# Ranking instructions by due time, a two-round selection for the first block, and three pieces of elementwise work moved to ScalarE, in a two-layer hybrid encoder

## The chip, the cores and the metric

The kernel runs on one core of one Trainium2 chip. The core has a matrix engine (TensorE, PE in the profile, with its weight loads as PEld), VectorE (DVE), ScalarE (ACT), GpSimd (POOL) and SyncE (SP, which issues the DMAs). Each engine works through its own list in the order in which the program gives it. The metric is the time of one execution on the device in microseconds (us).

## The reference, cut to what matters

The input is 512 frames of width 1024, with 16 learned meta tokens ahead of them. There are two layers, and after them a last normalization. In float32:

```python
# layer 1: sparse attention (8 heads) beside gated linear attention (4 heads)
score = einsum(relu(iq . ik), iw) * IDX_SCALE       # the indexer, per query over all keys
score = where(admissible, score, -1e30)
idx   = top_k(score, 128)                           # 128 keys for each query
logits = q . k[idx] / 8 + rel_bias                  # per head
p = softmax(where(ok, logits, -1e30)); oa = p @ v[idx]
ob = head_rms(gla_chunked(bq, bk, bv, log_a))
h = h + (concat(oa * silu(ag), ob * silu(bg)) @ w_out_ab)
# layer 2: retention (4 heads) beside stick-breaking attention (8 heads)
z = q . k / 8                                       # keys before the query only
log_1m = -softplus(z)                               # max(z,0) + ln(1 + exp(-|z|)), negated
w = exp(log_sigmoid(z) + (reverse_cumsum(log_1m) - log_1m)); od = w @ v
oc = head_layer_norm(retention(cq, ck, cv))
h = h + (concat(oc * silu(cg), od * silu(dg)) @ w_out_cd)
y = rms_norm(h)
```

Queries come in four blocks of 128. Block b sees 16 + 128(b+1) keys: 144, 272, 400 and 528.

## The kernel before

Every product in float32 accuracy is made of three: a weight tile `raw` (128x512) is split into a high part `wh` (a rounded copy made by ScalarE in `hi`) and a low part `wl` (`raw - wh`, made by VectorE in `lo`), the activations are split into `hh` and `hl` once per layer, and TensorE adds up hh.wh, hl.wh and hh.wl in a PSUM tile `acc` (two buffers). One projection of 128 columns is 8 such steps ("ticks"). Smaller products go to the PSUM tiles `x` (three buffers, shared by scores and transposes) and `y` (one).

Layer 1 plays its parts in the order of the string `V G0 G1 D A0 A1 C0 C1 A2 A3 C2 C3` after the indexer: values, two pairs of gated linear attention heads, the end of the selection (D), then four pairs of attention heads (A) and their gates (C). Layer 2 plays `V S0 S1 R0 S2 S3 R1`: S is a pair of stick-breaking heads, R a pair of retention heads. `out_ab` and `out_cd` are the out-projections.

**Selection** (`topk`). Each of the four blocks has a tile `score` (kind `lt`). A round finds the eight greatest of each row (`max`, which the trace shows as MAX8) and overwrites them with a mark (`match_replace`: MATCH_VALUE_LOAD and MATCH_REPLACE8). Sixteen rounds mark 128 keys; a last `tensor_scalar` turns marked into 0 and the others into -1e30, which the attention adds to its logits. The rounds of the four blocks take turns.

**Attention and stick-breaking** work on units: blocks 0 and 1 together (416 columns), block 2 (400), block 3 (528, in two PSUM tiles of 272 and 256). For softmax, ScalarE makes the exponentials with their sums, VectorE the reciprocal, and VectorE multiplies by it. For a stick-breaking unit, ScalarE makes |z| from PSUM, VectorE copies z out of PSUM and then makes max(z, 0) from the copy (tile `m`), ScalarE makes ln(1 + exp(-|z|)), VectorE adds up backwards over the keys (a scan that reads `m`), subtracts, and ScalarE exponentiates. Then TensorE transposes the weights and multiplies by the values.

**The order of the work.** No instruction is issued when the code calls it. A `Recorder` notes all of them in the order of the code (`o.at`), with their dependences; in that order chains of small steps are mixed into the projections by the tick. Two readers of one PSUM tile on different engines are noted as a dependence too. Then `order` plays a model of the five engines, with a cost for each instruction from `price`, and picks for each engine again and again the listed instruction with the least

```python
key = (max(est + (self.MARGIN if e == "tensor" else 0) - base, 0.0), o.pri)
```

where `est` is when the instruction could start by the model and `base` when the engine is free. Among instructions that could start at once, `o.pri` decides, and it is the place in the code. (The two subtractions from it in `add` are by `EVICT` and `SPLIT`, both 0.) Buffers of one kind are handed out in the order of the code. `issue` then emits everything in the order found; all of it has line 373 in the trace, so the trace is read by tile names.

Of the kernel before, what the change touches and what calls it, by code (L numbers as in the profile page):

```python
# [9 lines left out]
F32 = mybir.dt.float32  # L10
F32R = mybir.dt.float32r
I32 = mybir.dt.int32
AF = mybir.ActivationFunctionType
ALU = mybir.AluOpType
AX = mybir.AxisListType

P = 128
DM = 1024
KT = DM // P
NMETA = 16  # L20
# [5 lines left out]
NEG = -1e30  # L26
# [99 lines left out]
class RecordedPool:  # L126
# [4 lines left out]
    def tile(self, shape, dt, tag=None, bufs=1, name=None):  # L131
        fixed = tag is None
        tag = tag or name
        n = 1
        for y in shape[1:]:
            n *= y
        if tag not in self.kinds:
            k = self.kinds[tag] = Kind()
            width = max(n, {"tiny": 32, "mid": P}.get(tag, 0))
            k.width, k.pool, k.tag = width, self.pool, tag  # L140
            k.free = [(0.0, i) for i in range(bufs)]
            k.any = self.pool.tile(shape, dt, name=tag) if fixed else k.buffer(0, F32)
        k = self.kinds[tag]
        t = Held(k, shape, dt, self.psum, self.whole)
        t.width = k.width
        if fixed:
            t.fixed, t.buf = True, k.any
        return View(t, (), t.shaped(k.any))
# [17 lines left out]
class Recorder:  # L166
# [6 lines left out]
    def add(self, eng, name, args, kw):  # L173
        o = Op()
        o.eng, o.name, o.args, o.kw = eng, name, args, kw
        views = [x for x in args if isinstance(x, View)]
        outs = [x for x in args[:1] if isinstance(x, View)]
        if name == "tensor_tensor_reduce":
            outs.append(args[7])
        if isinstance(kw.get("accum_out"), View):  # L180
            outs.append(kw["accum_out"])
        ins = [x for x in list(args[1:]) + list(kw.values()) if isinstance(x, View) and not any(x is y for y in outs)]
        if name == "copy_predicated":
            ins.append(args[0])
        o.outs, o.ins = outs, ins
        o.at = o.pri = len(self.ops)
        kinds = {x.tile.kind.tag for x in outs + ins}
        if eng != "tensor":
            o.pri -= self.EVICT if "acc" in kinds else self.SPLIT if kinds & {"wh", "wl"} else 0
        o.preds, o.succs, o.tiles = {}, [], []  # L190
        for write, xs in ((False, ins), (True, outs)):
            for x in xs:
                self.depend(o, x, write)
        self.price(o)
        self.ops.append(o)
# [22 lines left out]
    def price(self, o):  # L218
        o.mm, o.port = None, False
        n = max([x.free() for x in o.ins + o.outs] or [1])  # L220
        sbuf = not any(x.tile.psum for x in o.ins)
        scalar = 65 if any(isinstance(x, View) and x.free() == 1 for x in o.ins) and n > 1 else 0
        if o.eng == "tensor":
            lhs, rhs = (o.args[1], o.args[2]) if len(o.args) > 2 else (o.kw["lhsT"], o.kw["rhs"])
            turn = o.name == "transpose"
            plain = rhs.dtype == F32
            k, m, n = lhs.shape[0], lhs.free(), rhs.free()
            two = plain and not turn
            o.mm = (k, plain, max(n * 0.452 * (2 if two else 1) + 2, 107 * m / P + 2) + (107 if two and n <= P else 0))
            o.cost = max(273, 170 + 0.4375 * n) if not two else 180 + 1.62 * n  # L230
        elif o.eng == "scalar":
            o.cost = (205 if sbuf else 165) + 0.83 * n + (80 if isinstance(o.kw.get("bias"), View) or isinstance(o.kw.get("scale"), View) else 0)
            if "accum_out" in o.kw:
                o.cost += 200
        elif o.eng == "vector":
            o.port = sbuf and o.name not in ("max", "match_replace")
            if o.name == "tensor_tensor_scan":
                o.cost = 144 + 2.1 * n
            elif o.name in ("tensor_scalar", "tensor_copy") and sbuf:
                o.cost = 160 + 0.52 * n + scalar  # L240
            elif o.name == "memset":
                o.cost = 100 + 0.3 * n
            else:
                o.cost = 148 + 1.05 * n + scalar
            if o.name == "tensor_tensor_reduce" or "accum_out" in o.kw:
                o.cost += 80
            if o.name == "match_replace":
                o.cost += 70
        elif o.eng == "gpsimd":
            o.cost = {"memset": 92 + 0.84 * n, "tensor_tensor": 178 + 2.17 * n}.get(o.name, 194 + 1.5 * n)  # L250
        else:
            x = o.outs[0] if o.outs else o.ins[0]
            kb = n * x.shape[0] / 256
            o.cost = 2000 + kb * (9 if any(y.tile.whole for y in o.outs + o.ins) else 3.5)
# [3 lines left out]
    OVER = {"vector": -84, "scalar": -103, "gpsimd": -60}  # L258
    SWITCH, ROWS = 86, 50
    MARGIN = 300  # L260
    EVICT = 0
    SPLIT = 0
    SLACK = {"tensor": 0, "vector": 0, "scalar": 0, "gpsimd": 0, "sync": 0}

    def order(self):
        ops = self.ops
        for o in ops:
            o.wait = len(o.preds)
            for q in o.preds:
                q.succs.append(o)  # L270
        ends = {}
        free = dict.fromkeys(self.LAT, 0.0)
        lists = {e: [] for e in self.LAT}
        last = None
        pool_until = 0.0
        begun = {}
        result = []

# [98 lines left out]
class Kernel:  # L377
# [488 lines left out]
    def topk(self):  # L866

        nc = self.nc
        for b in range(NB):
            nk = NMETA + P * (b + 1)  # L870
            nc.gpsimd.memset(self.score[b][0:64, nk - 64:nk], NEG)
        for r in range(TOPK // 8):
            for b in range(NB):
                nk = NMETA + P * (b + 1)
                sc = self.score[b][:, :nk]
                m8 = self.sm.tile([P, 8], F32, tag="m8", bufs=4, name=self.name("m8"))
                nc.vector.max(m8, sc)
                nc.vector.match_replace(sc, m8, sc, MARK)
                yield self.TOPY
        for b in range(NB):  # L880
            nk = NMETA + P * (b + 1)
            sc = self.score[b]
            nc.vector.tensor_scalar(sc[:, :nk], sc[:, :nk], -2e38, NEG, op0=ALU.is_gt, op1=ALU.mult)
            nc.gpsimd.memset(sc[0:64, nk - 64:nk], NEG)
            yield 1

# [223 lines left out]
    def attention_steps(self, p, qs, ks, kl, strips, gates):  # L1110
# [6 lines left out]
        def scores(odd, u, ws):  # L1117
# [28 lines left out]
            for i, (b, c0) in enumerate(blocks):  # L1146
                nk = NMETA + P * (b + 1)
                nc.vector.tensor_scalar(pm[:, b, odd], bm[:, c0:c0 + NMETA], sums[:, i:i + 1], None, op0=ALU.mult)
                c = slice(c0 + NMETA, c0 + nk)
                nc.vector.tensor_scalar(bm[:, c], bm[:, c], sums[:, i:i + 1], None, op0=ALU.mult)  # L1150
                ws[odd, b] = bm[:, c0:c0 + nk]
            if u == 0:
                s = self.s()
# [416 lines left out]
    def stick_steps(self, p, qs, ks, kl, gates):  # L1570
# [3 lines left out]
        def scores(odd, u, ws):  # L1574
            blocks, banks = self.UNITS[u]
            l, m, z = self.wt(), self.wt(), self.wt()
            w = sum(k1 - k0 for prods in banks for _, k0, k1 in prods)
            for s, at, prods in self.qk_banks(banks, qs[odd], ks[odd], kl[odd], frames=True):
                n = s.shape[1]
                c = slice(at, at + n)  # L1580
                s0 = 0
                for b, k0, k1 in prods:
                    s0 += k1 - k0
                    if k1 == NMETA + P * (b + 1):
                        nc.vector.tensor_tensor(s[:, s0 - P:s0], s[:, s0 - P:s0], self.strict, op=ALU.add)
                nc.scalar.activation(l[:, c], s, AF.Abs)
                nc.vector.tensor_copy(z[:, c], s)
                if at + n < w:
                    yield 1
            nc.vector.tensor_scalar(m[:, :w], z[:, :w], 0.0, None, op0=ALU.max)  # L1590
            nc.scalar.activation(l[:, :w], l[:, :w], AF.Exp, scale=-1.0)
            nc.scalar.activation(l[:, :w], l[:, :w], AF.Ln, bias=self.one[:, 0:1])
            for b, c0 in blocks:
                c = slice(c0, c0 + NMETA + P * (b + 1))
                mv, lv = m[:, c], l[:, c]
                nc.vector.tensor_tensor_scan(mv[:, ::-1], mv[:, ::-1], lv[:, ::-1], 0.0, ALU.add, ALU.add)
                ws[odd, b] = mv
            nc.vector.tensor_tensor(m[:, :w], z[:, :w], m[:, :w], op=ALU.subtract)
            nc.scalar.activation(m[:, :w], m[:, :w], AF.Exp)
            for b, c0 in blocks:  # L1600
                nc.vector.tensor_copy(pm[:, b, odd], m[:, c0:c0 + NMETA])
            yield 1
# [160 lines left out]
```

## Time and profile before

| | |
|---|---|
| time, median of 3 runs | 668.94 us (668.85 to 668.98) |
| profiled execution, its own time | 667.77 us |
| its span, first to last instruction | 666.0 us |
| PE busy | 635.4 us (95%), 4469 matmuls |
| PEld busy | 580.6 us (87%) |
| DVE busy | 507.4 us (76%) |
| ACT busy | 383.1 us (58%) |
| POOL busy | 74.9 us (11%) |
| mean granted TensorE clock | 0.988 |
| chain that ended last | PE 68%, DVE 17%, ACT 9%, issue 3% |

Busy time is the union of an engine's instructions. Matmuls are pipelined and overlap, so that a wait shorter than a matmul doesn't show as idle time of PE. A granted clock of 1.00 is TensorE's upper level (2.4 GHz), 0.50 its lower one (1.2 GHz); a stretch with a value between holds some of each.

### The profile page before, as it was taken

To read this page: it belongs to the slowest core of one execution; us is meant where nothing else is said; L and a number is where in the kernel's file an instruction comes from. 1 tells how busy PE (TensorE), PEld (TensorE's weight loads), DVE (VectorE), ACT (ScalarE), POOL (GpSimd) and SP (SyncE) were. 2 spreads that over 40 slices of the span, in tenths; PEclk is the share of its full clock that TensorE was granted. 3 is DMA by queue.
4 is the path that set the end of the run, shared out by engine and by line. 5 is a ranking of instruction groups with operands and counts; after the bars stand their busy time and mean duration, and the time that the engine had idled before them with its cause. 6 is when DMAs were issued, how large, how long until landed. Compare 5 with 4: busy or idle time off the path is not lost.

```text
span 666.0 us, 12243 instructions
## 1 busy us (share of the span) xinstructions
PE 635.4 (95%) x4469; PEld 580.6 (87%) x4469; DVE 507.4 (76%) x1273; ACT 383.1 (58%) x846; POOL 74.9 (11%) x124
## 2 busy tenths in 40 slices
PE   6999999899999999999999999998999999899996
PEld 5979999799889999999899898877888879887884
DVE  5767799999998879799532854999846799865543
ACT  4656663353335667586443765888554797644434
POOL 7000100120110010001211200000200000110030
PEclk8999999999999999999999999999999999799999
DMA  8437223223214222231242453121222213224403
GB/s 238 110 82 226 64 64 96 49 81 90 57 34 121 75 67 74 64 96 48 71 124 72 159 157 90 49 76 48 74 75 64 64 32 90 70 64 153 148 17 126
DMA packets 91103, 59.25 MB, mean 89 GB/s; under 512 B 7314, under 2 KB 81628, under 8 KB 91044
## 3 DMA queue, kind: packets, MB, share of 16 engines
q1 hardware_dynamic: 91044, 58.48, 30.5%
q8 instruction: 35, 0.57, 0.3%
q14 instruction: 24, 0.20, 0.1%
HBM read 53.18 MB, written 6.90 MB: 90 GB/s over the span
## 4 chain that ended last, share of the span: by engine, by line
PE 68%; DVE 17%; ACT 9%; issue 3%; DMA 1%; SPq 1%; POOL 0%; POOLq 0%; ACTq 0%; DVEq 0%
PE acc L373 46%; PE x L373 15%; PE y L373 6%; ACT wt L373 4%; DVE wt L373 3%; DVE lt L373 3%; DVE m L373 3%; DVE st L373 3%; DVE wl L373 2%; ACT st L373 2%; ACT wh L373 1%; SPq L373 1%; DVE pt L373 1%; DMA pt<-in_x_dram 1%; ACT pt L373 1%
## 5 line engine op out<-in xcount | busy, mean ns | idle before, releaser
L373 PE MATMUL acc<-hh,wh 128*128 128x272 f32 (+2 forms) x968 | 242.9, 312 | 1.7 <-DVE st L373 0.5
L373 PE MATMUL acc<-hl,wh 128*128 128x272 f32 (+2 forms) x968 | 234.9, 303 | 0.1
L373 PE MATMUL acc<-hh,wl 128*128 128x272 f32 (+2 forms) x968 | 233.0, 302 | 0.0
L373 ACT ACTIVATE wh<-raw 128x512 fp32r<-128x512 f32 x152 | 95.3, 629 | 124.6 <-PE acc L373 106.7
L373 PEld LDWEIGHTS acc<-hh,wh 128*128 128x128 f32 x968 | 158.2, 190 | 9.7 <-issue 1.4
L373 PEld LDWEIGHTS acc<-hh,wl 128*128 128x128 f32 x968 | 157.7, 189 | 5.6 <-issue 0.4
L373 PEld LDWEIGHTS acc<-hl,wh 128*128 128x128 f32 x968 | 157.7, 189 | 4.8 <-DVE hl L373 0.6
L373 DVE TENSOR_TENSOR wl<-raw,wh 128x512 fp32r<-128x512 f32 x153 | 111.0, 732 | 50.9 <-ACT wh L373 49.7
L373 POOL TENSOR_TENSOR gt<-gt,wt 128x528 f32<-128x528 f32 (+1 forms) x16 | 21.8, 1361 | 321.4 <-ACT wt L373 251.2
L373 PE MATMUL x<-ident,wt 128*128 128x128 f32 (+2 forms) x300 | 48.1, 278 | 7.7 <-DVE wt L373 4.5
L373 PE MATMUL x<-st,st 128*128 128x272 f32 (+6 forms) x240 | 50.9, 290 | 0.6 <-DVE pt L373 0.4
L373 ACT ACTIVATE wt<-x 128x272 f32<-128x272 f32 (+3 forms) x68 | 29.3, 434 | 34.3 <-PE x L373 22.4
L373 ACT ACTIVATE wt<-wt 128x528 f32<-128x528 f32 (+3 forms) x74 | 43.0, 593 | 9.2 <-DVE wt L373 8.4
L373 PEld LDWEIGHTS x<-ident,wt 128*128 128x128 f32 (+2 forms) x300 | 34.5, 140 | 15.5 <-DVE wt L373 6.7
L373 PEld LDWEIGHTS x<-st,st 128*128 128x128 f32 (+2 forms) x240 | 37.8, 187 | 6.5 <-DVE pt L373 1.3
L373 PE MATMUL y<-pt,vt 128*128 128x256 f32 (+1 forms) x288 | 39.7, 281 | 0.0
L373 PEld LDWEIGHTS y<-pt,vt 128*128 128x128 f32 x288 | 37.7, 195 | 0.1
L373 ACT ACTIVATE st<-acc 64x528 fp32r<-64x528 f32 (+1 forms) x58 | 34.7, 599 | 1.2 <-DVE lt L373 0.5
L373 DVE MATCH_REPLACE8 lt<-m,lt 128x144 f32<-128x144 f32 (+1 forms) x64 | 31.3, 493 | 0.2
L373 DVE TENSOR_TENSOR pt<-x,pt 128x384 fp32r<-128x384 f32 (+1 forms) x48 | 28.4, 595 | 3.9 <-ACT pt L373 3.5
L373 DVE TENSOR_TENSOR_SCAN wt<-wt,wt 128x64 f32<-128x64 f32 (+5 forms) x50 | 29.9, 634 | 1.1 <-ACT wt L373 1.0
L373 DVE MAX8 m<-lt 128x8 f32<-128x144 f32 (+1 forms) x64 | 30.1, 500 | 0.2
(188 smaller groups left out, 903.5 us busy)
## 6 DMA issues: line engine op xcount, KB each, us to landing
raw<-in_w_in_ab_dram SPq DMA_DIRECT2D x64, 256.0 KB, 2.8
raw<-in_w_in_cd_dram SPq DMA_DIRECT2D x56, 256.0 KB, 2.9
raw<-in_w_out_ab_dram SPq DMA_DIRECT2D x16, 256.0 KB, 2.7
raw<-in_w_out_cd_dram SPq DMA_DIRECT2D x16, 256.0 KB, 2.6
rep<-rows SPq DMA_DIRECT2D x8, 328.0 KB, 6.5
lt<-rep SPq DMA_DIRECT2D x8, 264.0 KB, 3.4
pt<-in_x_dram SPq DMA_DIRECT2D x8, 256.0 KB, 4.8
wt<-in_x_dram SPq DMA_DIRECT2D x8, 256.0 KB, 3.3
```

Source lines behind the costliest of these rows:

```text
L373: getattr(getattr(self.core, o.eng), o.name)(*[bind(x) for x in o.args], **{k: bind(x) for k, x in o.kw.items()})
```

## The change

Four things are changed.

1. `o.pri` becomes a due time. A new function `deadlines` lays the TensorE instructions one behind the other in the order of the code, which gives each a due time, and walks backward over all instructions: each must start early enough that those that need its result, and those that will take over its buffer, can start by their own times. TensorE instructions keep the place in the code as rank (their due times rise with it); all other engines, SP among them, rank by the latest start. What feeds no TensorE instruction gets its due time plus 20,000 ns.
2. The modelled cost of a matmul goes from 0.452 n + 2 to 0.455 n + 4 ns.
3. Block 0 has 144 keys, of which 128 are selected. Its scores are negated and reversed into a new tile `worst`, two rounds mark the 16 that are left out, and the last step reads `worst` reversed. The other blocks keep their 16 rounds.
4. The multiplication by the reciprocal of the softmax sum, and max(z, 0), go from VectorE to ScalarE. The latter now reads the PSUM tile, bank by bank, behind the copy of z.

```diff
-        kinds = {x.tile.kind.tag for x in outs + ins}
-        if eng != "tensor":
-            o.pri -= self.EVICT if "acc" in kinds else self.SPLIT if kinds & {"wh", "wl"} else 0
...
-            o.mm = (k, plain, max(n * 0.452 * (2 if two else 1) + 2, 107 * m / P + 2) + (107 if two and n <= P else 0))
+            o.mm = (k, plain, max(n * 0.455 * (2 if two else 1) + 4, 107 * m / P + 4) + (107 if two and n <= P else 0))
...
+    def deadlines(self):
+        ops, t, last = self.ops, 0.0, None
+        due = {}
+        for o in ops:
+            if o.eng == "tensor":
+                if last is not None:
+                    t += self.slot(last, o)
+                last = o
+            due[o] = t
+        late = {}
+        turn = {}
+        for o in reversed(ops):
+            end = min([late[q] - self.LAT[q.eng] for q in o.succs] + [late[q] - self.LAT[q.eng] for x in o.tiles
+                      for q in [turn.get((x.kind, x.at + x.kind.bufs))] if q and q.at > o.at], default=due[o] + 20000)
+            start = end - o.cost
+            if o.eng == "tensor":
+                start = min(start, due[o])
+            late[o] = start
+            for x in o.tiles:
+                turn[x.kind, x.at] = o
+        for o in ops:
+            o.pri = due[o] if o.eng == "tensor" else late[o]
...
+        self.deadlines()
...
+        sc = self.score[0][:, :NMETA + P]
+        worst = self.sm.tile([P, NMETA + P], F32, tag="worst", bufs=1, name="worst")
+        nc.vector.tensor_scalar(worst, sc[:, ::-1], -1.0, None, op0=ALU.mult)
+        def mark(x):
+            m8 = self.sm.tile([P, 8], F32, tag="m8", bufs=4, name=self.name("m8"))
+            nc.vector.max(m8, x)
+            nc.vector.match_replace(x, m8, x, MARK)
         for r in range(TOPK // 8):
             for b in range(NB):
...
+                if b == 0 and r >= (NMETA + P - TOPK) // 8:
+                    continue
+                mark(self.score[b][:, :NMETA + P * (b + 1)] if b else worst)
                 yield self.TOPY
...
-            nc.vector.tensor_scalar(sc[:, :nk], sc[:, :nk], -2e38, NEG, op0=ALU.is_gt, op1=ALU.mult)
+            if b:
+                nc.vector.tensor_scalar(sc[:, :nk], sc[:, :nk], -2e38, NEG, op0=ALU.is_gt, op1=ALU.mult)
+            else:
+                nc.vector.tensor_scalar(sc[:, :nk], worst[:, ::-1], -2e38, NEG, op0=ALU.is_lt, op1=ALU.mult)
...
-                nc.vector.tensor_scalar(bm[:, c], bm[:, c], sums[:, i:i + 1], None, op0=ALU.mult)
+                nc.scalar.activation(bm[:, c], bm[:, c], AF.Copy, scale=sums[:, i:i + 1])
...
                 nc.scalar.activation(l[:, c], s, AF.Abs)
                 nc.vector.tensor_copy(z[:, c], s)
+                nc.scalar.activation(m[:, c], s, AF.Relu)
...
-            nc.vector.tensor_scalar(m[:, :w], z[:, :w], 0.0, None, op0=ALU.max)
```

## Rows read from the trace of the kernel before

**Rows 1.** The page: span of the profiled execution.
```profile
span 666.0 us, 12243 instructions
```

**Rows 2.** Stretches: length; busy us of PE, PEld, DVE, ACT, POOL; clock; DMA share, GB/s.
```profile
8.60:14.90 6.30, 1.97 (x11) 1.16 (x11) 4.10 (x9) 3.65 (x13) 4.22 (x5) 0.79 0.97 273
60.00:80.00 20.00, 20.00 (x164) 19.99 (x163) 15.16 (x35) 11.74 (x27) 2.61 (x10) 1.00 0.38 94
80.00:200.00 120.00, 113.75 (x899) 107.22 (x898) 117.06 (x355) 51.76 (x114) 12.52 (x22) 1.00 0.27 68
200.00:320.00 120.00, 117.74 (x954) 115.05 (x954) 106.32 (x353) 79.76 (x188) 5.75 (x8) 1.00 0.27 76
418.00:438.00 20.00, 19.22 (x119) 16.56 (x119) 19.32 (x45) 19.63 (x41) 1.29 (x1) 1.00 0.14 41
460.00:466.00 6.00, 3.13 (x24) 2.51 (x22) 5.94 (x16) 4.81 (x11) 0.00 (x0) 1.00 0.16 48
566.00:576.00 10.00, 7.56 (x39) 6.96 (x38) 9.66 (x22) 6.43 (x14) 0.00 (x0) 0.66 0.24 66
```

**Rows 3.** Groups by shape: selection, block 0; last numbers: busy us, mean ns.
```profile
L373 DVE MAX8 m<-lt 128x8 f32<-128x144 f32 x16 | 4.8, 300 | 0.1
L373 DVE MATCH_REPLACE8 lt<-m,lt 128x144 f32<-128x144 f32 x16 | 4.7, 294 | 0.1
L373 DVE MATCH_VALUE_LOAD lt<-m,lt 128x8 f32 x64 | 5.1, 80 | 0.1
```

**Rows 4.** Timeline of DVE within the selection: start us, us.
```profile
188.16 0.30 DVE L373 MATCH_REPLACE8 lt<-m,lt 128x144 f32<-128x144 f32 x1
188.37 0.44 DVE L373 MAX8 m<-lt 128x8 f32<-128x272 f32 x1
```

**Rows 5.** Groups by shape: products with a per-row scalar, DVE and ACT.
```profile
L373 DVE TENSOR_SCALAR wt<-wt,tiny 128x512 f32<-128x512 f32 x8 | 3.8, 478 | 0.0
...
L373 DVE TENSOR_SCALAR wt<-wt,tiny 128x128 f32<-128x128 f32 x8 | 2.2, 280 | 0.0
L373 ACT ACTIVATE pt<-pt,tiny 128x512 f32<-128x512 f32 x4 | 2.9, 723 | 0.4
```

**Rows 6.** Groups by shape: max(z, 0) on DVE; ACT reading PSUM scores.
```profile
L373 DVE TENSOR_SCALAR wt<-wt 128x528 f32<-128x528 f32 x8 | 3.4, 429 | 0.1
L373 DVE TENSOR_SCALAR wt<-wt 128x416 f32<-128x416 f32 x8 | 3.0, 371 | 0.1
L373 DVE TENSOR_SCALAR wt<-wt 128x400 f32<-128x400 f32 x8 | 2.8, 354 | 0.1
L373 ACT ACTIVATE wt<-x 128x416 f32<-128x416 f32 x16 | 8.2, 513 | 17.6 <-PE x L373 13.5 <-DVE x L373 2.4 <-DVE lt L373 1.6
L373 ACT ACTIVATE wt<-x 128x400 f32<-128x400 f32 x16 | 7.9, 494 | 2.7 <-PE x L373 2.7
L373 ACT ACTIVATE wt<-x 128x272 f32<-128x272 f32 x16 | 6.3, 391 | 1.9 <-PE x L373 1.9
L373 ACT ACTIVATE wt<-x 128x256 f32<-128x256 f32 x16 | 6.1, 380 | 4.4 <-PE x L373 4.3
```

**Rows 7.** Chain that ended last, first stick pair: start us, us, what.
```profile
419.11 0.62 ACT wh L373
...
437.36 0.54 ACT wt L373
```

**Rows 8.** Timeline in the first and second stick pair: start us, us.
```profile
418.66 0.59 DVE L373 COPY wt<-x 128x416 f32<-128x416 f32 x1 [0.33 <-ACT wt L373]
...
455.08 0.48 ACT L373 ACTIVATE wt<-x 128x400 f32<-128x400 f32 x1
...
457.23 0.57 DVE L373 COPY wt<-x 128x400 f32<-128x400 f32 x1
```

**Rows 9.** Timeline of ACT at the start: start us, us, what ended its wait.
```profile
8.80 0.17 ACT L373 COPY gains<-x 128x18 f32<-128x18 f32 x1 [3.27 <-PE x L373]
```

More of the change, by code (lines that the diff above doesn't have):

```diff
@@ L139, in tile @@
             width = max(n, {"tiny": 32, "mid": P}.get(tag, 0))
+            k.bufs = bufs
             k.width, k.pool, k.tag = width, self.pool, tag
@@ L260 @@
     MARGIN = 300
-    EVICT = 0
-    SPLIT = 0
-    SLACK = {"tensor": 0, "vector": 0, "scalar": 0, "gpsimd": 0, "sync": 0}
+    def deadlines(self):
[20 more added lines that the diff above has]
+            o.pri = due[o] if o.eng == "tensor" else late[o]
     def order(self):
@@ L274, in order @@
         last = None
-        pool_until = 0.0
         begun = {}
@@ L871, in topk @@
             nc.gpsimd.memset(self.score[b][0:64, nk - 64:nk], NEG)
+        sc = self.score[0][:, :NMETA + P]
[5 more added lines that the diff above has]
+            nc.vector.match_replace(x, m8, x, MARK)
         for r in range(TOPK // 8):
             for b in range(NB):
[L874 to L878, printed above, removed]
+                if b == 0 and r >= (NMETA + P - TOPK) // 8:
+                    continue
+                mark(self.score[b][:, :NMETA + P * (b + 1)] if b else worst)
                 yield self.TOPY
```

## The prediction

> **What bounds the kernel now.** I read the page, then the stretches, because one busy share over the span hides that the stages have different limits. PE is busy 95% of the span, so only idle PE can be won back. The rest of the reading asks which engine PE waits for in each stretch.
>
> From 80 to 200 us VectorE is the limit: it is busy 117.06 of 120 us, ScalarE only 51.76, and PE's gaps sum to 120 - 113.75 = 6.25 us [rows 2]. This is the stretch of the selection, whose rounds run on VectorE beside the weight splits. In the attention stretch, 200 to 320 us, VectorE is still the busiest (106.32) but PE's gaps are only 2.26 us [rows 2]. In the first stick-breaking pair, 418 to 438 us, both VectorE (19.32 of 20) and ScalarE (19.63 of 20) are full [rows 2]. There the chain of work that ended last runs through ScalarE alone, from 419.11 to 437.90 us in some 40 pieces [rows 7]. At the end of each of the two runs of stick pairs PE stands still: 2.87 us between 460 and 466, 2.44 us between 566 and 576, and in the second case the granted clock then falls, to a mean of 0.66 over the 10 us, which is 6.8 us at 1.2 instead of 2.4 GHz [rows 2]. The last place is the start: from 8.60 to 14.90 us PE works 1.97 of 6.30 us [rows 2].
>
> The sum is made against the profiled execution: 666.0 us of span [rows 1] and 1.77 us around it, 667.77 us. The median of the runs is 1.17 us above that, so I add this at the end.
>
> **The change part by part.**
>
> *Selection.* Fourteen of block 0's sixteen rounds go. One round is MAX8 300 ns, MATCH_REPLACE8 294 ns and MATCH_VALUE_LOAD 80 ns [rows 3], together 674 ns, so 14 x 0.674 = 9.4 us. Consecutive VectorE instructions overlap: a MATCH_REPLACE8 of 300 ns is followed by the next instruction after 0.21 us [rows 4]. With some 0.08 us of overlap for each of three instructions a round holds the engine 0.45 to 0.5 us, so VectorE is really freed by about 7 us; the added pass for `worst`, a tensor_scalar of 144 columns, is about the 280 ns of the 128-column one [rows 5]. What is that worth? The lower end is nothing, if PE's waits there are each one instruction long and stay. The upper end is the 6.25 us of gaps. VectorE would fall from 117 to 110 of 120 us while PE needs 113.75 of them, so the limit passes to PE. Some gaps are single long instructions ahead of a short one and remain. I take -4 us, about two thirds.
>
> The Trainium skill (Perfetto Trace Analysis, Identifying the Most-Contended Engine) holds that the busy share of matmuls is a bad measure and names that of the weight loads instead. By the loads, 107.22 of 120 us against 19.99 of 20 in the stretch before [rows 2], the room is 12.8 us and not 6.25. The trace bears this out only where matmuls are short: from 418 to 438 us the loads read 16.56 and the matmuls 19.22 [rows 2], since a 512-column product hides its load. By the page the term would be up to -7 us, all that VectorE is freed by; I count it as the rival of a larger gain, below.
>
> *Division of the softmax.* 32 products leave VectorE: eight each of 512, 384, 256 and 128 columns, from 478 ns down to 280 ns [rows 5], on average 379 ns, 12.1 us. On ScalarE the same form, a copy with a per-row scale over 512 columns, takes 723 ns [rows 5]. ScalarE's slope is (513 - 380)/160 = 0.83 ns a column [rows 6], so 617, 510 and 404 ns for the smaller ones, 8 x 2.254 = 18.0 us in all. The stretch 200 to 320 holds it: ScalarE would go from 79.8 to 98 of 120 us, VectorE from 106 to 94. What stands behind it on ScalarE's list (exponentials, `wh` splits, evictions) now waits for a reciprocal on VectorE too. With gaps of 2.26 us little can be won, and one such wait per unit (24 units) of 0.1 us would cost as much. I take -0.5 us, between -2 and +3.
>
> *max(z, 0).* 24 instructions leave VectorE: 8 x (429 + 371 + 354) ns = 9.2 us. 32 come to ScalarE: 8 x (513 + 494 + 391 + 380) ns = 14.2 us [rows 6], 3.6 us for each of four pairs. It also stands differently. The copy of z waits for |z| on the other engine (0.33 us idle, ended by ScalarE) [rows 8], so one PSUM tile is read by one engine at a time. The new instruction must stand behind that copy. The copy itself can be late: |z| of one unit starts at 455.08 and its copy at 457.23 us [rows 8]. So the scan waits for ScalarE where it waited for its own engine, and the `x` tile is held 0.4 to 0.5 us longer, with scores and transposes of TensorE queued for it. In S0 and S2 the chain is ScalarE's already [rows 7], so most of 3.6 us lands on it; against that the new ranks can put off the two passes that finish a gate, which nothing needs soon, by about 1.3 us (two of 0.64 to 0.72 us by the 0.83 ns slope and the 723 ns row). That makes +2.2 us for each. In S1 and S3 VectorE is the fuller (5.94 of 6 us before the stall) [rows 2] and loses 2.3 us of work a pair; I take -1.2 us for each. Sum +2 us. Bounds: -6 (both end stalls, 2.87 and 2.44, go) and +14 (all that ScalarE takes on).
>
> *Ranks.* TensorE's own ranks stay in the order of the code, as due times only rise. On the other engines work that TensorE needs soon passes work with time to spare, which is what the selection stretch wants. At the start SP's transfers are ranked as well: a frame block needs a longer chain of work than the meta tokens, so frames can be issued ahead of them. ScalarE there waits 3.27 us for the gains with a block's square behind it [rows 9]. An order that puts this right wins up to the 4.3 us of PE's gaps between 8.60 and 14.90 [rows 2]; a worse one costs another wait of 3.3 us. I take -1 us. In the remaining stages (out-projections, retention) VectorE and ScalarE have room and most of the reordering is of work that isn't waited for: -1 us, between -3 and +3. The new matmul cost moves the model by 1 or 2% and is counted here.
>
> Sum: -4 - 0.5 + 2 - 1 - 1 = -4.5 us. 667.77 - 4.5 = 663.3, and with 1.17 to the median 664.4 us.
>
> **The rivals.**
>
> *A larger gain.* The freed VectorE time goes into PE in full (-7), the stall after S3 shrinks so far that the clock doesn't fall (6.8 us at half the clock give back up to 3.4), and the start gains 3: -13, with nothing lost in the stick pairs, 656 us. For it: the stall at 566 us ends on VectorE work, which gets 2.3 us less in that pair, and the stall at 460 us of 2.87 us was not followed by a fall [rows 2]. Against it: three things must all go well, and the relu adds to the other engine.
>
> *Slower: ScalarE binds the stick pairs.* Of the 14.2 us that ScalarE takes on, S0 and S2 put all of theirs on the chain (+7.1), S1 and S3 half (+3.6), and a longer stall at 460 us brings a fall of the clock such as the one after 566 us (+3.4): +14, less the 6.5 us gained elsewhere, 676 us. For it: ScalarE is at 19.63 of 20 us there. Against it: over both runs of stick pairs ScalarE has spare time later on, and the ranks can use it. It decides from the point where the stick pairs lose more than the 6.5 us that the other terms give. The same page and section of the Trainium skill, to improve the most contended engine, speaks for this rival: in this stretch the change loads the engine that is fullest by the trace.
>
> *No change.* The selection may not be on the path: its rounds already fill VectorE's idle time, and fewer of them leave PE waiting for the same `wl` splits and states one instruction at a time. Then -1.5 us from the start and the ranks meets +2 from the stick pairs: 669 us.
>
> **How the numbers follow.** A change under 0.2%, 1.3 us, is about what a measurement of this kernel can't tell from none. Chances: my forecast 0.45 (its own range 659 to 667.5), the larger gain 0.20, slower 0.23, no change 0.12. Faster is the first two and a little of the last: 0.66. Same: 0.08. Slower: 0.26. For the range, 653 takes in all but the best third of the larger gain, and 675 nearly half of the slower case: 653 to 675 us, with about 0.2 left out.
>
> **What would show it.** Between 80 and 200 us VectorE's busy share falls below 95% and PE's gaps below 3 us; the selection ends earlier than now. In the first stick pair ScalarE is full for longer and the chain stays on it; PE's gaps there grow from 0.8 us to 2 or 3. The attention stretch keeps its length with ScalarE near 98 of 120 us. The first products of layer 1 start before 14.9 us. I am wrong if PE's gaps in the selection stretch stay at 6 us, or if the stick pairs take more than 4 us longer or the granted clock falls at more places than now.

## The result, and the profile after

| | before | after |
|---|---|---|
| median of 5 runs, same chip | 668.98 us (668.85 to 670.67) | 663.56 us (662.72 to 665.88) |
| ratio, 95% interval | 1 | 0.9904 (0.9883 to 0.9924) |
| profiled execution, its own time | 667.77 us | 663.46 us |
| its mean granted clock | 0.988 | 0.984 |

The kernel is faster by 0.96% by the ratio in the table. The two medians alone give 0.9919, which lies inside the interval, so 0.8 to 1% is what can be said. 664.4 us had been forecast. The sum was right to 0.8 us, but several of its terms were wrong by more than that, two of them in sign, and they cancelled: that the number came out is luck.

The page after: span, busy times (share of the span, instructions), and the chain that ended last.

```profile
span 661.7 us, 12217 instructions
PE 636.6 (96%) x4469; PEld 581.4 (88%) x4469; DVE 484.3 (73%) x1176; ACT 405.1 (61%) x910; POOL 76.4 (12%) x124
PE 67%; DVE 18%; ACT 9%; issue 2%; DMA 2%; SPq 0%; DVEq 0%; ACTq 0%
```

VectorE gave 23 us away and ScalarE took 22, and none of it can be seen in the shares of the chain. The stretches tell more. The columns are those of [rows 2]; the seven rows that answer to it come first, then two of the stick-breaking stage and three around 120 us.

```profile
8.60:14.90 6.30, 1.46 (x10) 0.76 (x8) 6.21 (x12) 2.73 (x11) 5.46 (x5) 0.82 0.91 222
60.00:80.00 20.00, 20.00 (x163) 20.00 (x162) 14.77 (x28) 12.31 (x27) 3.17 (x10) 1.00 0.52 146
80.00:200.00 120.00, 114.56 (x882) 107.53 (x881) 112.55 (x318) 52.80 (x119) 12.61 (x23) 0.97 0.27 69
200.00:320.00 120.00, 119.24 (x970) 117.12 (x970) 96.13 (x318) 90.66 (x213) 5.83 (x8) 1.00 0.24 67
418.00:438.00 20.00, 19.96 (x125) 17.22 (x124) 16.97 (x39) 17.43 (x41) 0.00 (x0) 1.00 0.13 38
460.00:466.00 6.00, 6.00 (x49) 5.62 (x48) 5.94 (x16) 5.96 (x17) 0.00 (x0) 1.00 0.15 36
566.00:576.00 10.00, 10.00 (x83) 9.68 (x82) 9.94 (x20) 9.47 (x23) 1.60 (x1) 1.00 0.24 63
...
440.00:480.00 40.00, 38.53 (x266) 34.18 (x266) 38.38 (x79) 35.08 (x76) 6.49 (x6) 1.00 0.31 87
546.00:586.00 40.00, 39.37 (x272) 35.33 (x273) 36.44 (x76) 33.64 (x74) 6.91 (x6) 1.00 0.32 93
...
118.00:120.00 2.00, 1.66 (x13) 1.27 (x12) 1.99 (x6) 1.98 (x4) 0.00 (x0) 1.00 0.53 128
120.00:122.00 2.00, 0.29 (x2) 0.23 (x2) 1.97 (x7) 1.41 (x3) 0.48 (x1) 0.98 0.01 4
122.00:124.00 2.00, 2.00 (x9) 1.87 (x9) 2.00 (x5) 0.00 (x0) 1.30 (x2) 0.50 0.00 0
```

Three things stand out against [rows 2]. At the ends of the two runs of stick pairs, where PE stood still for 2.87 and 2.44 us, it now works 6.00 of 6.00 and 10.00 of 10.00 us, and the fall of the clock after 568 us is gone. In the selection stretch VectorE is 4.5 us less busy (112.55 for 117.06), but PE's gaps only went from 6.25 to 5.44 us, and the granted clock is 0.97 over the stretch: at 120 us PE stands still, and then the clock is at its lower level. The start is worse: 1.46 us of PE in 6.30, for 1.97.

A stretch between fixed times doesn't hold the same work in two kernels. For a balance I took the start of the n-th matmul into `acc`, of which every kernel here has 3008, and subtracted that of the kernel before. In us, each column the change within that part; one profiled execution of each:

| part (matmuls into `acc`; time before) | after | ranks alone | edits alone |
|---|---|---|---|
| start (to the first; 14.9) | +2.5 | +2.3 | +0.7 |
| up to the selection (to the 300th; 79.0) | +0.5 | +1.6 | +1.5 |
| selection (to the 1000th; 202.2) | +2.7 | +6.4 | -1.5 |
| attention and `out_ab` (to the 2100th; 400.9) | -2.6 | -2.2 | +2.3 |
| stick pairs (to the 2900th; 605.7) | -6.4 | -5.7 | +7.3 |
| the rest (to the last; 636.9) | -1.0 | -1.1 | 0.0 |
| sum | -4.3 | +1.3 | +10.4 |

"Ranks alone" and "edits alone" are the first two experiments. The profiled execution of the first is one with three falls of the clock (mean 0.977) and 2.3 us above its median; the sign of its sum is that of this execution.

How far a part moves by itself can be read from experiments 8, 9 and 12 below. Up to 419 us they have the instructions of the kernel before on every engine in the same order. Still their first four parts differ from its profile by -0.6 to -0.3, +1.2 to +2.6, +0.5 to +1.6 and 0.0 to -0.1 us. Each of them has a fall of the clock near 121 us (3.4, 6.8 and 6.8 us long) that the profile of the kernel before doesn't have; that profile has the highest mean clock (0.988) of all runs of its kernel here. So up to the 1000th matmul a change of 1 or 2 us in the table can't be told from none. The two parts behind it are firmer: in all nine kernels with due times there the attention part is 2.0 to 2.8 us and the stick pairs 5.7 to 7.7 us shorter than before.

### The profile page after: what moved, and what is told of

Same layout as the page of the kernel before. It is cut to its first block, busy times and chain, and to the rows that moved or that the text cites. A ratio compares the mean times of both kernels' runs of the same rounds, so it can differ in the third digit from the quotient of the medians.

```text
span 661.7 us, 12217 instructions
## 1 busy us (share of the span) xinstructions
PE 636.6 (96%) x4469; PEld 581.4 (88%) x4469; DVE 484.3 (73%) x1176; ACT 405.1 (61%) x910; POOL 76.4 (12%) x124
## 4 chain that ended last, share of the span: by engine, by line
PE 67%; DVE 18%; ACT 9%; issue 2%; DMA 2%; SPq 0%; DVEq 0%; ACTq 0%
PE acc L393 45%; PE x L393 15%; PE y L393 6%; ACT wt L393 6%; DVE wt L393 5%; DVE st L393 3%; DVE lt L393 3%; DVE wl L393 3%; DVE m L393 2%; DMA pt<-in_x_dram 2%; ACT pt L393 1%; DVE pt L393 1%; ACT ptm L393 1%; ACT st L393 0%; DVE vt L393 0%
## 5 line engine op out<-in xcount | busy, mean ns | idle before, releaser
L393 PE MATMUL acc<-hh,wh 128*128 128x272 f32 (+2 forms) x968 | 246.5, 315 | 3.0 <-ACT hh L393 1.5
L393 DVE TENSOR_TENSOR wl<-raw,wh 128x512 fp32r<-128x512 f32 x153 | 109.1, 718 | 57.2 <-ACT wh L393 52.2
L393 ACT ACTIVATE wt<-x 128x272 f32<-128x272 f32 (+3 forms) x100 | 43.0, 453 | 28.4 <-PE x L393 17.8
L393 PE MATMUL x<-ident,wt 128*128 128x128 f32 (+2 forms) x300 | 46.0, 275 | 2.1 <-DVE wt L393 1.2
L393 ACT ACTIVATE wt<-wt,tiny 128x272 f32<-128x272 f32 (+5 forms) x64 | 34.7, 561 | 10.3 <-DVE tiny L393 10.0
L393 ACT ACTIVATE wt<-wt,one 128x528 f32<-128x528 f32 (+3 forms) x42 | 29.5, 705 | 0.2
```

The source lines that it names most:

```text
L393: getattr(getattr(self.core, o.eng), o.name)(*[bind(x) for x in o.args], **{k: bind(x) for k, x in o.kw.items()})
```

## The experiments

The theory after the first comparison of the traces: the ranks gain in the stick pairs and in the attention; the selection's freed time is eaten by the stall at 120 us and the clock behind it; max(z, 0) on ScalarE costs nothing as long as the ranks stand. The rivals: the three edits carry the gain, by themselves; or the ranks hurt the start and the selection so much that they are better left off there.

**1. Ranks alone** (due times and the new matmul cost; the three edits of selection, division and max taken back).

```diff
-        nc.vector.tensor_scalar(worst, sc[:, ::-1], -1.0, None, op0=ALU.mult)
...
-                if b == 0 and r >= (NMETA + P - TOPK) // 8:
-                    continue
...
-                nc.scalar.activation(bm[:, c], bm[:, c], AF.Copy, scale=sums[:, i:i + 1])
+                nc.vector.tensor_scalar(bm[:, c], bm[:, c], sums[:, i:i + 1], None, op0=ALU.mult)
...
-                nc.scalar.activation(m[:, c], s, AF.Relu)
+            nc.vector.tensor_scalar(m[:, :w], z[:, :w], 0.0, None, op0=ALU.max)
```

> The kernel before with the due-time ranks and the new matmul cost alone. Theory A (the ranks keep TensorE fed in the stick-breaking stretch, which became 6.5 us shorter, and lose 2.5 us at the start): about 664 us, with the stick stretch (from the 2100th to the 2800th matmul into acc) 4 to 7 us shorter than before and the first product near 17.4 us. Theory B (the work taken from VectorE does it, the ranks only cost the start): about 671 us, stick stretch as before.

Measured: 0.9961 of the time before (0.9946 to 0.9977). Of the 0.96% the ranks, with the new matmul cost, give 0.39% by themselves. The time is between the two theories; the signs are those of theory A (stick pairs -5.7 us, first product at 17.2 us).

**2. Edits alone** (the order of the code and the old matmul cost, with the three edits).

```diff
-        self.deadlines()
...
-            o.mm = (k, plain, max(n * 0.455 * (2 if two else 1) + 4, 107 * m / P + 4) + (107 if two and n <= P else 0))
+            o.mm = (k, plain, max(n * 0.452 * (2 if two else 1) + 2, 107 * m / P + 2) + (107 if two and n <= P else 0))
```

> The three edits (selection in two rounds, relu and division on ScalarE) with ranks in the order of the code and the old matmul cost. Theory A: 667 to 671 us, the stick pairs not shorter, the first product at 14.9 us as before. Theory B: 659 to 662 us, that is the changed kernel without its loss at the start.

Measured: 1.0107 (1.0086 to 1.0127), slower. The two halves add up to +0.68%, and together they give -0.96%: the edits together need the ranks. The first rival falls, and the time is above what either theory had expected. Which of the three edits it is, experiment 8 shows.

**3. The change without max(z, 0) on ScalarE**; the fourth pair of lines of experiment 1.

> The changed kernel with max(z, 0) back on VectorE. Theory A, with ScalarE full in the stick pairs: 660 to 663 us, faster than the changed kernel by up to 3 us. Theory B: 666 to 669 us, because VectorE gets 9.2 us of work back in stretches where it is full, and the stalls at the end of the stick pairs come back.

Measured: 0.9905 (0.9885 to 0.9924), the same as the whole change. Under the ranks this edit is worth nothing, for better or worse.

**4. The change without the division on ScalarE**; the third pair of lines of experiment 1.

> The changed kernel with the division back on VectorE. If the parts add up under the new ranks (ranks alone 0.9961, selection about 0.004, relu nothing), what is left for the division is about 0.002: ratio 0.992 to 0.993, 664 to 666 us on a chip where before takes 669 to 670. If the division is worth nothing, as predicted to within 0.5 us: 0.990.

Measured: 0.9912 (0.9892 to 0.9933). Worth nothing that can be told from none.

**5. The change with all sixteen rounds for block 0**; the selection's lines of experiment 1.

> The changed kernel with sixteen rounds for block 0 again. If the fourteen rounds are worth what was predicted, 4 us, and only a fall of the clock near 122 us hid it: 666 to 668 us. If the selection is filler that fits into VectorE's idle time under the new ranks: 663 to 664 us, no change.

Measured: 0.9942 (0.9922 to 0.9962), 0.38% slower than the whole change, with intervals that just meet. So the rounds are worth some 2.5 us, give or take 2, and with the 0.39% of experiment 1 they account for 0.77 of the 0.96 percentage points.

**6. SP in the order of the code**, all else as after.

```diff
-            o.pri = due[o] if o.eng == "tensor" else late[o]
+            o.pri = due[o] if o.eng == "tensor" else o.at if o.eng == "sync" else late[o]
```

> The changed kernel with SP alone ranked by the place in the code. Theory S (the ranks of the transfers cause the loss at the start, where the first product comes 2.5 us later): the first product between 14 and 15.5 us, total 1.5 to 3 us under the changed kernel, ratio near 0.987. Rival (the ranks of ScalarE and VectorE at the start, or the place where the clock falls, cause it): first product still after 16.5 us, ratio 0.990.

Measured: 0.9887 (0.9866 to 0.9909), 0.17% better than after, with overlapping intervals. The place where it should act is clear in the trace: the first matmul into `acc` starts 0.16 us later than before, not 2.5.

**7. Ranks only from the attention on**; up to the place where part A0 begins all engines go by the code.

```diff
+            o.pri = due[o] if o.eng == "tensor" else late[o] if o.at >= self.cut else due[o] + 1e-3 * o.at
...
+            if p == "A0":
+                self.nc.cut = len(self.nc.ops)
```

> The changed kernel with ranks by the place in the code up to the first attention pair (start, indexer, values, gated linear attention, most of the selection) and due times behind it. If the ranks lose in the selection stretch (from the 300th to the 1000th matmul into acc 2.7 us more than before, while the three edits without the ranks take 1.6 us less) and at the start, and win in the attention and the stick pairs: 656 to 660 us, ratio 0.981 to 0.986. If stretches don't combine so: 662 to 666 us.

Measured: 0.9903 (0.9879 to 0.9927), as after. The start is repaired (first matmul +0.27 us), yet the selection part is 5.0 us longer than before: two stalls for `attm`, 3.7 us together, and a fall of the clock behind each. So leaving the ranks off up to there doesn't take the loss in the selection away, and the second rival falls for it. The new matmul cost is still in this run.

**8. max(z, 0) on ScalarE alone**, in the kernel before.

```diff
                 nc.vector.tensor_copy(z[:, c], s)
+                nc.scalar.activation(m[:, c], s, AF.Relu)
...
-            nc.vector.tensor_scalar(m[:, :w], z[:, :w], 0.0, None, op0=ALU.max)
```

> The kernel before with max(z, 0) on ScalarE from PSUM and nothing else. The three edits without the ranks lost 7.3 us between the 2100th and the 2900th matmul into acc. If the relu does that in the order of the code: 673 to 678 us, ratio 1.007 to 1.012, with the loss in that stretch. If it comes from the changed time at which the stretch begins or from the clock: 668 to 671 us.

Measured: 1.0137 (1.0114 to 1.016), a little over the expected range. The balance puts 7.7 us of it into the stick pairs. This is the whole loss of experiment 2. The stretches of the stick pairs in this kernel, and in the kernel before:

```profile
440.00:480.00 40.00, 36.14 (x233) 32.95 (x233) 32.57 (x67) 31.50 (x69) 3.62 (x4) 0.93 0.26 73
546.00:586.00 40.00, 34.42 (x222) 30.46 (x221) 33.41 (x70) 33.55 (x73) 2.56 (x2) 0.96 0.24 67
```

```profile
440.00:480.00 40.00, 36.91 (x246) 32.09 (x246) 36.78 (x77) 28.84 (x59) 4.99 (x5) 1.00 0.26 73
546.00:586.00 40.00, 37.56 (x238) 33.63 (x236) 35.53 (x74) 28.13 (x58) 4.96 (x5) 0.91 0.26 74
```

Neither engine is full in the slower kernel: VectorE 32.57 and ScalarE 31.50 of 40 us. PE waits more: 13.6 us in all between 418 and 590 us, for 7.3 before.

**9. max(z, 0) on ScalarE from the copy of z**, in the kernel before: the PSUM tile `x` is not held by it.

```diff
-            nc.vector.tensor_scalar(m[:, :w], z[:, :w], 0.0, None, op0=ALU.max)
+            nc.scalar.activation(m[:, :w], z[:, :w], AF.Relu)
```

> The kernel before with max(z, 0) on ScalarE, made from the copied z in SBUF in one pass per unit, where VectorE made it. The load on ScalarE is about that of the relu from PSUM (8 x (643 + 545 + 528) ns = 13.7 us against 14.2 us), but the PSUM tile is free as early as before. Theory L (ScalarE's full list in the order of the code costs the 7 us): 674 to 679 us, as with the relu from PSUM. Rival H (the PSUM tile held longer costs them): 668 to 671 us.

Measured: 1.0107 (1.0076 to 1.0137), and 7.9 us in the stick pairs. It costs about the same without the hold of `x`, so rival H falls as the whole cause. The load by itself isn't the cause either, since about the same load costs nothing under the ranks (experiment 3). What is left is the order in which the engines take their work; which instructions of it make the loss, no run isolates. The two kernels lose differently. In experiment 8 the four waits for `wt` of ScalarE end with the new pass itself, which frees the tile `x` late; in 9 these are gone, and PE waits for VectorE's copies of z and for ScalarE's gate passes out of `acc`. PE's waits between 418 and 590 us (us in all, times, longest us), the two largest groups, first of experiment 8, then of 9:

```profile
PE x L373 <- DVE ptm L373: 4.9, 2, 2.4
PE x L373 <- ACT wt L373: 4.6, 4, 1.5
```

```profile
PE x L373 <- DVE wt L373: 4.8, 6, 1.9
PE acc L373 <- ACT wt L373: 3.3, 4, 1.0
```

**10. Old matmul cost and SP in the order of the code**, all else as after: the edit of experiment 6 with

```diff
-            o.mm = (k, plain, max(n * 0.455 * (2 if two else 1) + 4, 107 * m / P + 4) + (107 if two and n <= P else 0))
+            o.mm = (k, plain, max(n * 0.452 * (2 if two else 1) + 2, 107 * m / P + 2) + (107 if two and n <= P else 0))
```

> The changed kernel with SP in the order of the code and the old modelled cost of a matmul (0.452 n + 2 ns). All runs that lost in the selection stretch (300th to 1000th matmul into acc) had the new cost; the only one that gained there had the old cost and the old ranks. If the cost does it: 656 to 659 us, ratio 0.981 to 0.985, without a fall of the clock near 120 us. If the cost is worth nothing: 661 us, ratio 0.988 to 0.990.

Measured: 0.9854 (0.9827 to 0.9881), 659.72 us, the fastest version of all, better than both kernels. Against experiment 6 the intervals overlap; that the old cost is the better one is likely and not settled. The sign that the theory named did not come: the clock still falls at 119.3 us, and the selection part is +2.2 us. What is better than in experiment 6 is mostly the stick pairs, with -7.7 us for -6.4. The new cost was not run without the ranks.

**11. A selection round only where nothing else can start** within 700 ns by the model, with SP in the order of the code. The theory was that rounds which fill VectorE's gaps stand in the way of what the plan has late.

```diff
-                    key = (max(est + (self.MARGIN if e == "tensor" else 0) - base, 0.0), o.pri)
+                    wait = self.MARGIN if e == "tensor" else 700 if o.name in ("max", "match_replace") else 0
+                    key = (max(est + wait - base, 0.0), o.pri)
```

> The changed kernel with SP in the order of the code, and MAX8 and MATCH_REPLACE8 chosen for VectorE only when by the model nothing else can start within 700 ns. Theory F (rounds of the selection put in front of a short instruction that TensorE waits for make the stall near 120 us, after which the clock falls): the wait for attm shrinks below 1 us, no fall of the clock near 120 us, 656 to 659 us. Rival (VectorE runs behind the model by more than one instruction there, whatever is filled in): the stall and the fall stay, 660 to 662 us.

Measured: 0.9894 (0.9866 to 0.9921). The wait for `attm` is still 1.9 us, and the clock still falls at 120.7 us. This theory falls.

**12. Late gates**, in the kernel before: in a stick pair the last three steps of the gate (logarithm, exponential, product) are put 22 ticks later in the code. The theory was that the ranks gain in the stick pairs by putting off just these.

```diff
+        def rest():
+            nc.scalar.activation(e[:, c], e[:, c], AF.Ln, bias=self.one[:, 0:1])
+            nc.scalar.activation(e[:, c], e[:, c], AF.Exp, scale=-1.0)
+            nc.gpsimd.tensor_tensor(t[:, c], t[:, c], e[:, c], op=ALU.mult)
...
+            self.chains.insert(0, [self.now + 22, rest(), None])
```

> The kernel before, in the order of the code, with the last two ScalarE passes and the product of each stick gate put 22 ticks later in the code, about where the due times put them (443.5 us instead of 425.2 us for the first pair). Theory G (what the ranks win in the stick pairs is mostly these passes getting out of the way): the stretch from the 2100th to the 2900th matmul into acc 3 to 6 us shorter than before, 663 to 666 us. Rival (the win comes from the order of all the rest, unit against unit, splits, evictions): 0 to 1.5 us, 667 to 669 us.

Measured: 1.0011 (0.9992 to 1.0029), no gain. It is a weak test of the theory. The exponential moved to 437.35 us, but the logarithm still starts at 428.54 us, in the middle of the pair's chain. The order takes first what can start first, so a later place in the code alone doesn't hold an instruction back; the theory isn't settled by it.

## Why the prediction came out right, step by step

**Stick pairs: +2 us forecast, -6.4 us measured.** This is the largest miss, and two terms of it failed. The first is the help of the ranks, put at 1.3 us for each of S0 and S2, by two gate passes put off. They are worth far more than that: with max(z, 0) still on VectorE they take 5.7 us from the stick pairs (ranks alone). The second is the sentence that put "most of 3.6 us" of each of S0 and S2 onto ScalarE's chain. In the order of the code there is a loss (experiments 8 and 9: +7.7 and +7.9 us in the stick pairs, in profiles with 3.4 and 6.8 us more at the lower clock there), about half of the +14 us of the rival in which ScalarE binds, and without ScalarE being full; under the ranks there is none (experiment 3). The signs named for the first pair didn't come: ScalarE is busy 17.43 of 20 us there, and PE's gaps are 0.04 us instead of 2 or 3. PE's waits between 418 and 590 us (us in all, times, longest us), before and after:

```profile
PE x L373 <- DVE wt L373: 4.5, 7, 1.7
PE x L373 <- DVE ptm L373: 1.6, 2, 0.8
PE acc L373 <- DVE st L373: 0.5, 2, 0.3
```

```profile
PE acc L393 <- DVE wl L393: 1.9, 2, 1.0
PE x L393 <- DVE pm L393: 0.9, 2, 0.5
```

The seven waits for `wt` of VectorE are gone, and with them the stalls at the pairs' ends. What they waited for was a free `x` tile: each ends with a copy of z out of PSUM. The one at the end of the first run of stick pairs, before (start us, us, what PE waited for):

```profile
459.61 0.38 ACT L373 ACTIVATE wt<-x 128x272 f32<-128x272 f32 x1
461.77 0.42 DVE L373 COPY wt<-x 128x272 f32<-128x272 f32 x1
462.25 0.55 PE L373 MATMUL x<-ident,wt 128*128 128x128 f32 x3 [1.65 <-DVE wt L373]
```

The copy starts 2.16 us after |z| of the same tile, behind a maximum, a subtraction and a scan of other units on VectorE's list; the stall of 1.68 us after S3 has the same form. Over the 32 tiles of z in the stick pairs the copy starts 1.29 us after |z| on the mean in the kernel before, 1.24 in experiment 9, and 0.71 in experiments 1 and 3. The prediction had seen a late copy [rows 8] and charged it to the new pass; that the ranks would bring the copy forward it didn't reckon. The fall of the clock that followed the second stall in [rows 2] (6.8 us at 1.2 GHz, up to 3.4 us) went too; the forecast had this only in the rival of a larger gain. That the gates are put off is seen: the logarithm of S0's gate starts at 425.22 us before and at 443.50 us after (timeline of ScalarE, start us, us).

```profile
425.22 0.72 ACT L373 ACTIVATE wt<-wt,one 128x512 f32<-128x512 f32 x1
```

```profile
443.50 0.71 ACT L393 ACTIVATE wt<-wt,one 128x512 f32<-128x512 f32 x1
```

It is one of many moves, and no run here shows how much of the 5.7 us is its share; late gates in the code (experiment 12) gave none.

The size of the moved work was right: the eight extra passes of each shape raise ScalarE's time on PSUM scores from 28.5 us [rows 6] to 43.6 (12.2 + 12.0 + 9.8 + 9.6), 15.1 us where 14.2 were reckoned. That is a sum of durations, and on an engine they overlap: ScalarE's busy time, 405.1 us, is only 8.7 us above that of experiment 3.

```profile
L393 ACT ACTIVATE wt<-x 128x400 f32<-128x400 f32 x24 | 12.2, 517 | 2.9 <-PE x L393 2.9
L393 ACT ACTIVATE wt<-x 128x416 f32<-128x416 f32 x24 | 12.0, 517 | 13.0 <-PE x L393 8.8 <-DVE x L393 2.4 <-DVE lt L393 1.6
L393 ACT ACTIVATE wt<-x 128x272 f32<-128x272 f32 x24 | 9.8, 410 | 1.9 <-PE x L393 1.9
L393 ACT ACTIVATE wt<-x 128x256 f32<-128x256 f32 x24 | 9.6, 402 | 4.3 <-PE x L393 4.2
```

**Selection: -4 us forecast, some -2.5 measured for the rounds, and a loss beside it that wasn't foreseen.** The rounds are worth 0.38% (experiment 5); the mechanism was right, and the share of PE's gaps that they would close was put too high. That they free VectorE by about 7 us was right: it is busy 484.3 us, for 491.3 with all rounds. (The prediction's own overlap, 0.674 - 0.24 = 0.43 us a round, would have made 6 us.) VectorE's share between 80 and 200 us fell below 95% as expected (93.8%), but PE's gaps stayed above 3 us (5.44), near the 6 us that the prediction had named as a sign against itself. The selection doesn't end earlier than before either: its last step ends at 194.2 us in both kernels, and at 206.0 us under the ranks with all rounds. What is left of the gaps is to a good part one wait. The timeline of VectorE and PE after (start us, us, in brackets PE's wait and what ended it), and PE's longest wait of that kind before:

```profile
120.06 1.53 DVE L393 MAX8 m<-lt 128x8 f32<-128x272 f32 x3
121.50 0.14 DVE L393 COPY_PREDICATED attm<-tri,x 16x16 f32<-16x16 int32 x1
121.71 0.22 PE L393 MATMUL x<-ident,st 64*16 64x64 f32 x1 [2.04 <-DVE attm L393]
```

```profile
117.79 0.22 PE L373 MATMUL x<-ident,st 64*16 64x64 f32 x1 [1.23 <-DVE attm L373]
```

A 0.14 us copy stands behind three MAX8, and PE waits 2.04 us for it. Behind that wait the clock is at half for 6.8 us. Such a fall doesn't need the change: experiments 8, 9 and 12, with the order of the kernel before up to there, have one at the same place after waits of 1.2 to 1.3 us. Experiments 9 and 12, in which it lasts 6.8 us, have a selection part 1.6 and 1.0 us longer than that of the kernel before. So of the +2.7 us after, 1 to 2 us remain when order is compared with order under the same fall.

What takes back the rounds' gain there is open. Ranks alone have +6.4 us (with two falls), sixteen rounds under the ranks +4.0 (one short fall), the edits without ranks -1.5 (none), which speaks for the ranks or the new matmul cost. But experiment 7, without ranks up to the attention, has +5.0 (two falls), and experiment 10, with the old cost, +2.2 (one). The wait for `attm` is in every profile: 1.2 to 1.3 us in the order of the kernel before, 1.6 with the edits alone, 1.8 to 2.1 in all others, with margin for the rounds (experiment 11) or without. Why VectorE comes to that copy late is open too.

The rule of the Trainium skill that the prediction weighed here (Perfetto Trace Analysis, Identifying the Most-Contended Engine: judge TensorE's headroom by the busy share of the weight loads, or by its share of the peak arithmetic) would have given up to -7 us by the loads. The trace doesn't agree: the loads read 107.53 of 120 us after and 107.22 before [rows 2], though VectorE was freed by 7 us, and between 418 and 438 us they read 17.22 of 20 while the matmuls read 19.96 and PE hardly waits.

**Start: -1 us forecast, +2.5 measured.** Wrong in sign. The five profiles with the transfers by due time (after, experiments 1, 3, 4 and 5) have +1.2 to +2.7 us, the eight others -0.6 to +0.7. The prediction saw that frames could be issued ahead of the meta tokens and took that for a chance. It is a loss, as the timelines of SP, ScalarE and PE show, after:

```profile
2.61 0.89 SPq L393 DMA_DIRECT2D gv<-in_meta_tokens_dram  x2
7.14 0.63 ACT L393 ACTIVATE wt<-gv 16x512 f32<-16x512 f32 x1 [5.11 <-DMA gv<-in_meta_tokens_dram]
...
16.23 0.63 ACT L393 ACTIVATE wh<-raw 128x512 fp32r<-128x512 f32 x1 [2.79 <-DMA raw<-in_w_in_ab_dram]
16.77 1.23 ACT L393 ACTIVATE hh<-x,gains 128x272 fp32r<-128x272 f32 x3
17.38 0.79 PE L393 MATMUL acc<-hh,wh 128*128 128x272 f32 x2 [1.52 <-ACT hh L393]
```

and before:

```profile
0.75 0.86 SPq L373 DMA_DIRECT2D gv<-in_meta_tokens_dram  x2
2.55 0.63 ACT L373 ACTIVATE wt<-gv 16x512 f32<-16x512 f32 x1 [0.52 <-DMA gv<-in_meta_tokens_dram]
14.27 1.24 ACT L373 ACTIVATE hh<-x,gains 128x272 fp32r<-128x272 f32 x3 [1.55 <-PE x L373]
14.90 0.57 PE L373 MATMUL acc<-hh,wh 128*128 128x272 f32 x1 [0.24 <-ACT hh L373]
```

The meta tokens are issued 1.86 us later, behind four frame transfers, and their first use starts 4.59 us later; their square is the first piece of work on ScalarE's list in both kernels, so nothing else starts there until 7.14 us. Later a `wh` split stands ahead of the first `hh` on the list and waits 2.79 us for its `raw`, where before `hh` went first. So the wait of 3.27 us in [rows 9] did go (`gains` starts without a wait), as hoped, and two others took its place. With SP in the order of the code both are gone and the loss with them (experiment 6), though `gains` waits again: the other engines' ranks stayed, so it was the transfers.

**Division: -0.5 us forecast, nothing that can be told from none measured** (experiment 4). Right as far as can be told, and so were the durations of its working. The products of each size, after (busy us, mean ns), in the stretch from 200 to 320 us, where one of the eight of 512 columns is missing:

```profile
L393 ACT ACTIVATE wt<-wt,tiny 128x512 f32<-128x512 f32 x7 | 5.0, 721 | 0.1
...
L393 ACT ACTIVATE wt<-wt,tiny 128x384 f32<-128x384 f32 x8 | 4.9, 610 | 0.7 <-DVE tiny L393 0.6
...
L393 ACT ACTIVATE wt<-wt,tiny 128x256 f32<-128x256 f32 x8 | 3.9, 493 | 0.0
...
L393 ACT ACTIVATE wt<-wt,tiny 128x128 f32<-128x128 f32 x8 | 3.2, 396 | 1.3 <-DVE tiny L393 1.1
```

8 x (721 + 610 + 493 + 396) ns = 17.8 us; 18.0 had been reckoned from a slope and one row. The waits for a reciprocal (`tiny`) that were feared are 0.6 and 1.1 us in all, on an engine that is busy 90.66 of 120 us there. The prediction had 98: it added up durations, which overlap, and over the whole kernel the division makes ScalarE busy for 13.7 us more (405.1, for 391.4 in experiment 4).

**Other ranks: -1 us forecast, about -3.6 measured** (-2.6 in the attention and `out_ab`, -1.0 at the end). Right in sign and too small. Ranks alone have -2.2 and -1.1 in the same parts.

**The sum.** By parts it is +2.5 + 0.5 + 2.7 - 2.6 - 6.4 - 1.0 = -4.3 us, forecast -4.5. The forecast got there with a gain in the selection and at the start and a loss in the stick pairs; it was the other way round, and that the two sums agree is luck. What the prediction missed is one thing: it priced each edit by itself and the ranks as a small correction to them, where the ranks decide what the edits cost.

## What to carry to other kernels

Moving work to another engine is priced by the order that it is put into, not by the engine's spare time: the same 32 instructions cost 1.37% in one order and nothing in another, and neither engine was full in the slow case. A wait that the profile puts down to a tile of another engine can be a wait for a buffer: look at what the releasing instruction reads, here a PSUM tile that it frees. Where an order by due time is brought in, look at the transfers separately: a transfer that gets ahead of one that the consumers' lists need first moves the wait to the head of every list behind it. And where a forecast is right in its sum, balance it part by part all the same.

## What the runs showed of the hardware that wasn't expected

The clock's falls go with much of the spread between runs. Of 20 runs of the kernel before on one chip the ten at a mean granted clock of 0.986 took 668.6 to 670.0 us, and the eight at 0.978 or 0.979 took 670.5 to 672.4. So a single profile can show a fall that the median doesn't have, or lack one that it has, and a stretch's length is to be read together with its clock. The lower level came in pieces of 3.4 to 13.7 us in these profiles, and the same stall isn't always followed by one: the wait of 1.23 us for `attm` was followed by none in the profile of the kernel before, and by 3.4 us at the lower level in experiment 8, with the same order up to there. And where VectorE is the fullest engine, a piece of 6.8 us cost well under half of its length: the selection part of the kernel before was 1.0 and 1.6 us longer with one (experiments 12 and 9).
